# The second product of a feed forward as seven products of quarters

## The chip, the cores and the metric

The kernel runs on one core of a Trainium2 chip. The metric is the device time of one execution in microseconds. The engines are PE (matrix products), DVE (vector), ACT (scalar), POOL (GpSimd) and SP, which here only issues transfers; an engine that issues a transfer does so from a queue of its own.

## The reference

Two decoder layers on 512 tokens of 1024 channels. Each has three token mixers (pooling, an S5 state space, sparse attention), a merge, a layer norm, and then the feed forward, whose last two lines are what most of the change touches:

```python
for i in range(DEPTH):        # DEPTH = 2
    proj = x @ w_in           # then pool_mixer, s5_mixer, nsa_mixer on parts of proj
...
x = layer_norm(ALPHA * x + merged @ w_out, ln1_g, ln1_b)
h = jnp.square(jax.nn.relu(x @ w_ff1)) @ w_ff2      # 1024 -> 4096 -> 1024
return layer_norm(ALPHA * x + h, ln2_g, ln2_b)
```

Everything is in fp32.

## The kernel before, in words

An fp32 product is made of three matmuls of a shorter type. Each operand is split into a high part, rounded by a cast, and a low part, the remainder; `mm3_` (L98 to L100) sums high x high, high x low and low x high in PSUM. So each matrix costs a cast on ACT and a subtraction on DVE before PE can take it, and each 128x512 piece of a result costs three matmuls per 128 channels that are summed over.

Weights come through `wload` (L69 to L87): SP loads 512 KB into a staging tile `wst` (2 buffers), ACT casts it to `wh` (L82), DVE subtracts to get `wl` (L85); `wh` and `wl` have 4 buffers each. PSUM has 8 banks: `mm` 3, `s` 2, `t` 2, `o` 1.

The feed forward (`ffn` L1093, `feed_forward` L1224) goes through the 4096 hidden channels in 8 chunks of 512. `up(c)` makes the four hidden tiles of a chunk: 24 matmuls each, relu on ACT, square on DVE (L1103), split on ACT and DVE (`hi_lo`, L61, L62). `down(c)` multiplies the chunk with its 512 rows of the second weight matrix: for each half of the output channels and each block of 128 tokens `part` makes 12 matmuls and DVE adds the tile into the running sum `xs` (L1120). The loop issues `up(c + 1)` ahead of `down(c)`, and so PE always has products of the one or the other kind. The last chunk is done block by block, with the layer norm of a finished block beside the products of the next.

A tile framework puts each engine's instructions into an order of its own, by priorities; after that an engine executes in order, and each instruction waits for its operands and its buffers by semaphores.

Beside the feed forward of layer 0 stand two preparations for layer 1. `s5_ahead` (L535) lets POOL compute the operands of layer 1's S5 stage and store them to DRAM in four blocks `s5d`, one for each r; `wload` fetches the first four weights of layer 1's input projection at chunk 2. At the start of layer 1, `front(r)` in `s5_` loads a block back into `zwe` and transposes it on PE (L589). It is a generator that is advanced between other work: the number that it yields (L584: 10 for the first block, 3 for the others) says how many steps of the projection go ahead of it. A step is three matmuls.

Of the kernel before, what the change touches and what calls it, by code (L numbers as in the profile page):

```python
# [9 lines left out]
F32 = mybir.dt.float32  # L10
R = mybir.dt.float32r
# [7 lines left out]
DEPTH = 2  # L19
# [7 lines left out]
class Kern:  # L27
# [40 lines left out]

    def wload(self, ap, pool=None, split=None):  # L69
# [421 lines left out]
    def s5_operands(self, pool, i, r, zwe, eng, alone=False):  # L491
# [43 lines left out]
    def s5_ahead(self, i, after):  # L535

        with self.tc.tile_pool(name=f"s5a{i}", bufs=1, reuse_waits="tile") as pool:
            qs = [self.t(pool, [128, 3328], F32, f"zwe{k}") for k in range(2)]
            for r in range(5):
                with self.tc.issue_after(after):  # L540
                    if r < 2:
                        self.nc.gpsimd.memset(qs[r][:, 0:2304], 0.0)
                    if r < 4:
                        self.s5_operands(pool, i, r, qs[r % 2], self.nc.gpsimd, True)
                if r:
                    with self.tc.issue_after(self.loaded):
                        self.nc.sync.dma_start(self.s5d[r - 1], qs[(r - 1) % 2])
                yield

    def s5_(self, i):  # L550
# [5 lines left out]
        with tc.tile_pool(name=f"s5{i}", bufs=1, reuse_waits="tile") as sp:  # L556
# [21 lines left out]
            def front(r):  # L578
# [4 lines left out]
                Km = Ks[r % 2]  # L583
                yield 3 if r else 10  # L584
                lqs = []
# [506 lines left out]

    def ffn(self, i, xs, p0):  # L1093

        nc, v = self.nc, self.nc.vector

        def up(c):
            hs = []
            for m in range(4):
                ps = p0[m] if c == 0 else self.xw([self.wload(self.A["wf1"][i, 4 * c + m])])[0]  # L1100
                h = self.t(self.mt, [128, 512], F32, "mt")
                nc.scalar.activation(h, ps, AF.Relu)
                v.tensor_tensor(h, h, h, OP.mult)  # L1103
                hh, hl = self.pair("ab"[c % 2])
                self.hi_lo(hh, hl, h)
                hs.append((hh, hl))
            return hs

# [21 lines left out]
        def down(c, hs, post):  # L1130
            W = self.A["wf2"]
            if c < 7:
                for half in range(2):
                    ws = [None] * 4
                    for kp in range(2):
                        ws[2 * half + kp] = self.wload(W[i, c, half, kp])
                    for tb in range(4):
                        part(hs, ws, tb, half, c)
            else:
                ws = [self.wload(W[i, c, half, kp]) for half in range(2) for kp in range(2)]  # L1140
                return blocks(hs, ws, post)
# [82 lines left out]
    def feed_forward(self, i, xs, p0, w0p, g, b):  # L1224
        nc, A = self.nc, self.A
        up, down = self.ffn(i, xs, p0)
        how = ("aa", "aa", "am", "vv")
# [13 lines left out]
        for c in range(8):  # L1241
            nx = up(c + 1) if c < 7 else None
            if c == 1 and i < DEPTH - 1:
                ahead = self.s5_ahead(i + 1, self.affine.ins)
            if 1 <= c < 7 and i < DEPTH - 1:
# [9 lines left out]
            block = down(c, hs, post)  # L1255
            hs = nx
        if i < DEPTH - 1:
# [101 lines left out]
```

## Time and profile before

| what | us |
|---|---|
| median of 3 runs | 1772.05 |
| lowest and highest | 1771.15, 1772.34 |
| the profiled execution | 1768.97 |
| its span | 1767.2 |
| layer 0's feed forward | about 565 to 905 |
| layer 1's feed forward | about 1413 to 1751 |

The profile has the busy time of each engine, the chain of work that ended last, groups of instructions by line and form, what an engine waited for, and busy times by windows of the span. Matmuls are pipelined: one starts before the one ahead of it has ended, so the mean time of one is longer than the step from one to the next.

### The profile page before, as it was taken

To read this page: it belongs to the slowest core of one execution; us is meant where nothing else is said; L and a number is where in the kernel's file an instruction comes from. 1 tells how busy PE (TensorE), PEld (TensorE's weight loads), DVE (VectorE), ACT (ScalarE), POOL (GpSimd) and SP (SyncE) were. 2 spreads that over 40 slices of the span, in tenths; PEclk is the share of its full clock that TensorE was granted. 3 is DMA by queue.
4 is the path that set the end of the run, shared out by engine and by line. 5 is a ranking of instruction groups with operands and counts; after the bars stand their busy time and mean duration, and the time that the engine had idled before them with its cause. 6 is when DMAs were issued, how large, how long until landed. Compare 5 with 4: busy or idle time off the path is not lost.

```text
span 1767.2 us, 22544 instructions
## 1 busy us (share of the span) xinstructions
PE 1672.5 (95%) x8356; PEld 1397.7 (79%) x8356; DVE 1135.8 (64%) x2171; ACT 711.8 (40%) x1245; POOL 546.2 (31%) x636
## 2 busy tenths in 40 slices
PE   3969999999999999999998999999999999999996
PEld 2857887887779888888897788878787888888885
DVE  8797568676578656444576565867657774444447
ACT  2444336666534323233242442555564433222221
POOL 4993421322113999400033233122202050000002
PEclk9989999999999999999998999999999999999998
DMA  5313251111251246443316424211124133333331
GB/s 193 117 37 98 87 184 60 57 51 60 87 188 36 93 143 190 138 139 97 113 61 205 164 88 150 87 60 60 56 88 161 43 119 96 96 97 100 101 97 59
DMA packets 64334, 183.69 MB, mean 104 GB/s; under 512 B 12256, under 2 KB 21216, under 8 KB 63200
## 3 DMA queue, kind: packets, MB, share of 16 engines
q1 hardware_dynamic: 61632, 176.88, 30.9%
q10 hardware_dynamic: 2592, 5.38, 1.0%
q8 instruction: 65, 1.06, 0.3%
q14 instruction: 45, 0.37, 0.1%
HBM read 164.93 MB, written 17.30 MB: 103 GB/s over the span
## 4 chain that ended last, share of the span: by engine, by line
PE 78%; DVE 12%; POOL 4%; DMA 3%; ACT 2%; issue 1%; SPq 0%; DVEq 0%; ACTq 0%; POOLq 0%
PE mm L98 16%; PE mm L99 16%; PE mm L100 16%; PE s L99 4%; PE s L100 4%; PE s L98 4%; PE t L99 3%; PE t L100 3%; PE t L98 3%; PE o L834 3%; PE t L929 2%; DVE wl L85 1%; PE s L901 1%; PE s L900 1%; PE o L801 1%
## 5 line engine op out<-in xcount | busy, mean ns | idle before, releaser
L82 ACT CAST wh<-wst 128x1024 fp32r<-128x1024 f32 (+1 forms) x260 | 270.4, 1042 | 545.7 <-PE s L100 210.9
L85 DVE TENSOR_TENSOR wl<-wst,wh 128x1024 fp32r<-128x1024 f32 (+2 forms) x212 | 281.0, 1327 | 253.0 <-ACT wh L82 252.6
L98 PE MATMUL mm<-xh,wh 128*128 128x512 f32 (+1 forms) x1088 | 429.8, 395 | 6.6 <-ACT wh L82 5.4
L100 PE MATMUL mm<-xh,wl 128*128 128x512 f32 (+1 forms) x1088 | 420.2, 386 | 7.5 <-DVE wl L85 7.5
L99 PE MATMUL mm<-xl,wh 128*128 128x512 f32 (+1 forms) x1088 | 419.1, 385 | 0.0
L100 PEld LDWEIGHTS mm<-xh,wl 128*128 128x128 f32 x1088 | 205.5, 189 | 50.1 <-DVE wl L85 8.8
L98 PEld LDWEIGHTS mm<-xh,wh 128*128 128x128 f32 x1088 | 205.8, 189 | 44.9 <-ACT wh L82 5.9
L99 PEld LDWEIGHTS mm<-xl,wh 128*128 128x128 f32 x1088 | 206.0, 189 | 33.8
L85 POOL TENSOR_TENSOR wl<-wst,wh 128x1024 fp32r<-128x1024 f32 x48 | 122.2, 2546 | 239.2 <-ACT wh L82 233.5
L193 POOL TENSOR_TENSOR xm<-xm,ln_g 128x512 f32<-128x512 f32 x9 | 12.2, 1367 | 321.2 <-ACT xm L192 321.2
L906 ACT ACTIVATE P<-P,mx 128x512 f32<-128x512 f32 (+3 forms) x128 | 71.3, 559 | 63.5 <-DVE mx L904 63.0
L904 DVE CUSTOM_DVE_ANT_0 P<-s,mask 128x512 f32<-128x512 f32 (+3 forms) x128 | 59.6, 484 | 45.3 <-PE s L901 38.1
L62 DVE TENSOR_TENSOR Pl<-t,Ph 128x384 fp32r<-128x384 f32 (+1 forms) x96 | 57.3, 597 | 35.8 <-ACT Ph L61 35.5
L1120 DVE TENSOR_TENSOR xm<-xm,t 128x512 f32<-128x512 f32 x56 | 38.4, 686 | 54.1 <-PE t L100 51.2
L222 POOL TENSOR_TENSOR xm<-xm,hi_a 128x512 f32<-128x512 f32 x8 | 12.7, 1585 | 180.5 <-PE t L238 180.5
L222 POOL TENSOR_TENSOR xm<-xm,ln_g 128x512 f32<-128x512 f32 x16 | 30.2, 1886 | 121.6 <-PE t L238 121.6
L1120 DVE TENSOR_TENSOR xm<-xm,s 128x512 f32<-128x512 f32 x56 | 38.2, 682 | 41.6 <-PE s L100 41.6
L913 POOL TENSOR_SCALAR P<-P,sm,gate 128x128 f32<-128x128 f32 x32 | 15.3, 479 | 156.2 <-DVE sm L908 156.2
L61 ACT CAST Ph<-t 128x384 fp32r<-128x384 f32 (+1 forms) x96 | 48.1, 505 | 26.2 <-PE t L929 26.1
L98 PE MATMUL mm<-hi_a,wh 128*128 128x512 f32 x132 | 54.7, 414 | 2.1 <-DVE lo_a L318 2.1
L1103 DVE TENSOR_TENSOR mt<-mt 128x512 f32<-128x512 f32 x64 | 55.6, 869 | 0.0
L929 PE MATMUL t<-ident,P 128*128 128x128 f32 x320 | 51.8, 276 | 2.7 <-DVE P L913 2.7
(406 smaller groups left out, 3834.3 us busy)
## 6 DMA issues: line engine op xcount, KB each, us to landing
wst<-in_wf_dram SPq DMA_DIRECT2D x128, 512.0 KB, 3.5
wst<-in_win_dram SPq DMA_DIRECT2D x80, 512.0 KB, 3.3
wst<-in_wup_dram SPq DMA_DIRECT2D x24, 512.0 KB, 3.5
wst<-in_wout_dram SPq DMA_DIRECT2D x16, 512.0 KB, 4.2
s5d<-zwe SPq DMA_DIRECT2D x4, 1664.0 KB, 9.2
zwe<-s5d SPq DMA_DIRECT2D x4, 1664.0 KB, 9.1
xd<-xm SPq DMA_DIRECT2D x8, 512.0 KB, 4.9
w<-in_w_dram SPq DMA_DIRECT2D x8, 512.0 KB, 7.6
```

Of the source, the lines that this page charges most:

```text
L62: b = self.nc.vector.tensor_tensor(lo, src, hi.bitcast(F32), OP.subtract)
L82: self.nc.scalar.copy(wh, st)
L85: e.tensor_tensor(wl, st, wh.bitcast(F32), OP.subtract)
L98: mm(out, ah, bh, start=first and i == 0, stop=False, **kw)
L99: mm(out, ah, bl, start=False, stop=False, **kw)
L100: mm(out, al, bh, start=False, stop=last and i == n - 1, **kw)
L834: mm = lambda o, a, b, **k: nc.tensor.matmul(o, a, b, skip_group_check=True, **k)
L904: v.tensor_tensor_reduce(out=p, in0=ss[qb], in1=self.mask[:, 384 - 128 * qb:512], scale=-1.0, scalar=3e38, op0=OP.add, op1=OP.min, accum_o ...
L906: nc.scalar.activation(p, p, AF.Exp, bias=mx[:, qb:qb + 1], scale=-1.0, accum_out=c)
L929: nc.tensor.transpose(pt[:, n:n + 128], P[:, c:c + 128], self.ident)
L1103: v.tensor_tensor(h, h, h, OP.mult)
L1120: v.tensor_tensor(r, r, ps, OP.add)
```

## The change

A chunk that is `fast` (chunks 0 to 6 of layer 1; 0, 5 and 6 of layer 0) computes `down` as a product of 2x2 blocks in the seven products of Strassen's scheme in Winograd's form. The blocks of the hidden activations are quarters (256 channels x 256 tokens in two pieces of 128 channels), the blocks of the weights are the four loaded pieces. Four sums of the weights and four of the activations are formed on DVE in fp32 and then split; each product goes to two PSUM tiles, and DVE adds them into `xs` and into two tiles `AU`, which hold a term that three of the four output quarters have in common and are added to those at chunk 6. The raw weight pieces stay in four buffers of `big`, and are summed in place there.

Besides, the square of the hidden tile moves from DVE to ACT in all chunks. Twelve weights (the last chunk's four in both layers, the first four of layer 1's input projection) get `wl` in another way (`sums=True`): ACT writes the negated weight to it, rounded as in `wh`, and a transfer on POOL's queue adds the exact weight from DRAM, which leaves the remainder. The small S5 loads and the S5 stores of `s5_ahead` go from SP's to POOL's queue, in four steps instead of six. The first four weights of layer 1 are loaded at chunk 7. The affine part of the layer norm takes the blocks in another order, and the first S5 block of layer 1 yields 18 instead of 10.

```diff
     def wload(...)
+            if sums:
+                self.nc.scalar.activation(wl, st, AF.Copy, scale=-1.0)
+                self.nc.gpsimd.dma_start(wl, ap, accum_op=OP.add)
+                return wh, wl
...
-            for r in (rs[3], rs[0], rs[1], rs[2]):
+            for r in (rs[3], rs[2], rs[0], rs[1]):
...
-        nc.sync.dma_start(bc, self.A["s5bc"][i, :, :, r * 64:(r + 1) * 64])
+        (gl if alone else nc.sync).dma_start(bc, self.A["s5bc"][i, :, :, r * 64:(r + 1) * 64])
...
+                    self.nc.gpsimd.dma_start(self.s5d[r], qs[r % 2])
...
-                yield 3 if r else 10
+                yield 3 if r else 18 if i else 10
...
+        fast = lambda c: c < 7 and (i == DEPTH - 1 or c in (0, 5, 6))
+        def hidden(c, m, h):
+            ps = p0[m] if c == 0 else self.xw([self.wload(self.A["wf1"][i, 4 * c + m])])[0]
+            nc.scalar.activation(h, ps, AF.Relu)
+            nc.scalar.activation(h, h, AF.Square)
...
+            p11, p12, p22 = (split(q, self.pair("ab"[c % 2])) for q in (a11, a12, a22))
+            v.tensor_tensor(a22, a22, a21, OP.subtract)
+            e1 = esplit(a22, 1)
+            v.tensor_tensor(a21, a11, a21, OP.subtract)
+            v.tensor_tensor(a11, a11, a22, OP.add)
+            v.tensor_tensor(a12, a11, a12, OP.subtract)
+            e4 = esplit(a12, 4)
+            e3 = esplit(a21, 3)
+            e2 = esplit(a11, 2)
...
+        def products(c, hs):
...
+                b11, b12, b21, b22 = load(0, 0), load(1, 0), load(0, 1), load(1, 1)
+                w11 = split(b11)
+                add(b11, b12)
+                t1 = split(b11)
+                w21 = split(b21)
+                w22 = split(b22)
+                add(b12, b22)
+                t3 = split(b12)
+                add(b11, b22)
+                t2 = split(b11)
+                add(b11, b21)
+                t4 = split(b11)
...
+            mul(p11, w11, A)
+            if c == 0:
+                for j in range(2):
+                    v.tensor_copy(AU[j], A[j])
+            else:
+                acc(u, A, plus)
+            mul(e1, t1, C)
+            acc(lambda j: r(3, j), C, minus)
+            mul(p12, w21, A, False)
+            acc(lambda j: r(0, j), A, plus)
+            mul(e4, w22, C, False)
+            acc(lambda j: r(1, j), C, minus)
+            D, B = [self.psum("o"), self.psum("s")], [self.psum("s"), self.psum("t")]
+            mul(e3, t3, D)
+            acc(lambda j: r(3, j), D, minus)
+            mul(e2, t2, B)
+            acc(u, B, minus)
+            mul(p22, t4, D, False)
+            acc(lambda j: r(2, j), D, plus)
...
-            if c == 2 and i < DEPTH - 1:
-                w0 = [self.wload(A["win"][i + 1, j], w0p, nc.vector) for j in range(4)]
+            if c == 7 and i < DEPTH - 1:
+                w0 = [self.wload(A["win"][i + 1, j], w0p, sums=True) for j in range(4)]
...
+            if c == 6:
+                self.w7 = [self.wload(A["wf2"][i, 7, half, kp], w7, sums=True) for half in range(2) for kp in range(2)]
```

`load` brings a raw piece into `big` over SP, `split` casts on ACT and subtracts on DVE, `mul` makes 12 matmuls into two PSUM tiles (with `False` on top of what is there), and `acc` adds two tiles.

DVE in the middle of layer 1's feed forward, before: splits of weights (`wl`, 1024 columns), additions of tiles to `xm` (the tiles of `xs`), and a square and a remainder for each hidden tile.

```order
L85 TENSOR_TENSOR wl_14656<-wst_14653,wh_14655 128x1024
L85 TENSOR_TENSOR wl_14694<-wst_14691,wh_14693 128x1024
L1103 TENSOR_TENSOR mt_14570<-mt_14570 128x512
L62 TENSOR_TENSOR lo_a_14574<-mt_14570,hi_a_14573 128x512
L85 TENSOR_TENSOR wl_14700<-wst_14697,wh_14699 128x1024
L1103 TENSOR_TENSOR mt_14608<-mt_14608 128x512
L62 TENSOR_TENSOR lo_a_14612<-mt_14608,hi_a_14611 128x512
L85 TENSOR_TENSOR wl_14762<-wst_14759,wh_14761 128x1024
```

The same place now, around the start of a chunk's products; L1158 is a split of a weight block or sum, L1161 a sum of weight blocks, L1187 an accumulation.

```order
L1158 TENSOR_TENSOR wl_14330<-wh_14316,wh_14329 128x1024
L1161 TENSOR_TENSOR wh_14316<-wh_14316,wh_14322 128x1024
L62 TENSOR_TENSOR lo_a_14285<-wl_14150,hi_a_14284 128x512
L1158 TENSOR_TENSOR wl_14334<-wh_14320,wh_14333 128x1024
L1158 TENSOR_TENSOR wl_14338<-wh_14322,wh_14337 128x1024
L1187 TENSOR_TENSOR au_2500_13170<-au_2500_13170,s_14356 128x512
L1187 TENSOR_TENSOR au_2501_13171<-au_2501_13171,s_14357 128x512
L62 TENSOR_TENSOR lo_a_14289<-wl_14217,hi_a_14288 128x512
L62 TENSOR_TENSOR lo_a_14293<-wl_14217,hi_a_14292 128x512
L1187 TENSOR_TENSOR xm_12491<-xm_12491,t_14358 128x512
L1158 TENSOR_TENSOR wl_14343<-wh_14318,wh_14342 128x1024
```

The squares are gone, and sums and accumulations stand between the splits.

SP over one chunk in the same stretch, before: four loads of the first weight matrix, four of the second, all into `wst`.

```order
L79 DMA wst_2672_14251<-in_wf1_dram 128x1024
L79 DMA wst_2679_14289<-in_wf1_dram 128x1024
L79 DMA wst_2686_14327<-in_wf1_dram 128x1024
L79 DMA wst_2693_14365<-in_wf1_dram 128x1024
L79 DMA wst_2700_14403<-in_wf2_dram 128x1024
L79 DMA wst_2703_14409<-in_wf2_dram 128x1024
L79 DMA wst_2710_14471<-in_wf2_dram 128x1024
L79 DMA wst_2713_14477<-in_wf2_dram 128x1024
```

Now, the loads of one chunk:

```order
L79 DMA wst_2751_14463<-in_wf1_dram 128x1024
L79 DMA wst_2755_14496<-in_wf1_dram 128x1024
L1152 DMA wh_2782_14628<-in_wf2_dram 128x1024
L1152 DMA wh_2783_14630<-in_wf2_dram 128x1024
L1152 DMA wh_2784_14632<-in_wf2_dram 128x1024
L1152 DMA wh_2785_14634<-in_wf2_dram 128x1024
L79 DMA wst_2760_14530<-in_wf1_dram 128x1024
L79 DMA wst_2764_14563<-in_wf1_dram 128x1024
```

The four loads of the second matrix go to four buffers of their own, and stand between the second and the third load of the first matrix.

PE at the first S5 block of layer 1, before: `mm` tiles are the projection, `t` the transposes of `zwe`.

```order
L100 MATMUL mm_8657<-xh_1552_8024,wl_8654 128x512
L98 MATMUL mm_8657<-xh_1552_8024,wh_8653 128x512
L99 MATMUL mm_8657<-xl_1553_8025,wh_8653 128x512
L100 MATMUL mm_8657<-xh_1552_8024,wl_8654 128x512
L589 MATMUL t_8664<-ident_81,zwe_1613_8573 128x128 x4
```

Now:

```order
L103 MATMUL mm_8753<-xl_1587_8121,wh_8749 128x512
L104 MATMUL mm_8753<-xh_1586_8120,wl_8750 128x512
L102 MATMUL mm_8799<-xh_1584_8118,wh_8795 128x512
L103 MATMUL mm_8799<-xl_1585_8119,wh_8795 128x512
L104 MATMUL mm_8799<-xh_1584_8118,wl_8796 128x512
L590 MATMUL t_8806<-ident_81,zwe_1645_8669 128x128 x4
```

Before, one tile of 24 matmuls and 6 of the next (`mm_8657`) stand between the 128x256 products and the transposes; now two tiles (`mm_8753` the second) and 6 of the third (`mm_8799`).

## Rows read from the trace of the kernel before

**Rows 1.** The page, busy time of the engines and the chain that ended last.

```profile
PE 1672.5 (95%) x8356; PEld 1397.7 (79%) x8356; DVE 1135.8 (64%) x2171; ACT 711.8 (40%) x1245; POOL 546.2 (31%) x636
...
PE 78%; DVE 12%; POOL 4%; DMA 3%; ACT 2%; issue 1%; SPq 0%; DVEq 0%; ACTq 0%; POOLq 0%
```

**Rows 2.** Windows: stretch, length, busy us of PE, PEld, DVE, ACT, POOL, clock, DMA.

```profile
609.00:652.00 43.00, 43.00 (x191) 35.59 (x191) 21.47 (x24) 12.58 (x16) 42.17 (x77) 1.00 0.31 99
1413.00:1751.00 338.00, 337.98 (x1535) 281.41 (x1534) 178.33 (x222) 100.42 (x128) 30.59 (x19) 1.00 0.30 94
```

**Rows 3.** Instructions by form, PE, 1460 to 1740 us: busy, mean ns, idle before.

```profile
L98 PE MATMUL mm<-xh,wh 128*128 128x512 f32 x192 | 74.7, 389 | 0.0
```

**Rows 4.** Timeline of PE, layer 1's feed forward: start us, duration us.

```profile
1534.28 0.39 PE L99 MATMUL t<-wl,hi_a 128*128 128x512 f32 x1
...
1535.87 0.39 PE L100 MATMUL t<-wh,lo_a 128*128 128x512 f32 x1
```

**Rows 5.** Instructions by form, DVE, 1460 to 1740 us.

```profile
L85 DVE TENSOR_TENSOR wl<-wst,wh 128x1024 fp32r<-128x1024 f32 x51 | 62.4, 1223 | 84.7 <-ACT wh L82 84.7
L1120 DVE TENSOR_TENSOR xm<-xm,t 128x512 f32<-128x512 f32 x26 | 17.9, 687 | 26.9 <-PE t L100 26.5
...
L62 DVE TENSOR_TENSOR lo_b<-mt,hi_b 128x512 fp32r<-128x512 f32 x12 | 8.3, 692 | 6.2 <-ACT hi_b L61 6.2
```

**Rows 6.** Timeline of DVE, three instructions that follow on each other.

```profile
1544.18 1.23 DVE L85 TENSOR_TENSOR wl<-wst,wh 128x1024 fp32r<-128x1024 f32 x1 [1.76 <-ACT wh L82]
1545.32 0.68 DVE L1120 TENSOR_TENSOR xm<-xm,s 128x512 f32<-128x512 f32 x1
1545.92 1.22 DVE L85 TENSOR_TENSOR wl<-wst,wh 128x1024 fp32r<-128x1024 f32 x1
```

**Rows 7.** Instructions by form, ACT, 1460 to 1740 us.

```profile
L82 ACT CAST wh<-wst 128x1024 fp32r<-128x1024 f32 x50 | 52.7, 1054 | 159.0 <-PE s L100 100.6 <-PE mm L99 58.4
L1102 ACT ACTIVATE mt<-mm 128x512 f32<-128x512 f32 x24 | 14.1, 589 | 0.0
L61 ACT CAST hi_b<-mt 128x512 fp32r<-128x512 f32 x12 | 7.5, 622 | 16.8 <-DVE mt L1103 16.8
```

**Rows 8.** Instructions by form, DVE and POOL, 609 to 690 us in layer 0.

```profile
L85 DVE TENSOR_TENSOR wl<-wst,wh 128x1024 fp32r<-128x1024 f32 x18 | 24.8, 1377 | 23.3 <-ACT wh L82 23.3
...
L1120 DVE TENSOR_TENSOR xm<-xm,t 128x512 f32<-128x512 f32 x7 | 4.8, 683 | 6.3 <-PE t L100 4.1 <-POOL Wc L463 2.1
...
L62 DVE TENSOR_TENSOR lo_b<-mt,hi_b 128x512 fp32r<-128x512 f32 x4 | 3.3, 818 | 0.0
...
L461 POOL TENSOR_TENSOR ct<-Wc,s_are 128x128 f32<-128x128 f32 x6 | 4.7, 777 | 0.2
```

**Rows 9.** DMA issues: KB each, median us from issue to landing.

```profile
wst<-in_wf_dram SPq DMA_DIRECT2D x128, 512.0 KB, 3.5
...
s5d<-zwe SPq DMA_DIRECT2D x4, 1664.0 KB, 9.2
```

**Rows 10.** Windows, a stretch of dense loads; share and GB/s stand last.

```profile
240.00:254.00 14.00, 14.00 (x64) 11.58 (x63) 13.67 (x23) 3.47 (x6) 4.36 (x6) 1.00 0.97 337
```

**Rows 11.** What PE waited for, 900 to 1100 us: total, times, longest.

```profile
PE t L589 <- DMA zwe<-s5d: 5.8, 1, 5.8
```

**Rows 12.** Timeline of PE around the first S5 transposes of layer 1.

```profile
932.33 0.39 PE L100 MATMUL mm<-xh,wl 128*128 128x512 f32 x1
938.54 1.97 PE L589 MATMUL t<-ident,zwe 128*128 128x128 f32 x8 [5.82 <-DMA zwe<-s5d]
```

**Rows 13.** Windows behind that gap; the granted clock is third from last.

```profile
935.00:940.00 5.00, 1.46 (x7) 1.46 (x8) 2.19 (x4) 0.31 (x1) 3.23 (x2) 0.56 1.00 414
940.00:945.00 5.00, 5.00 (x27) 3.84 (x26) 1.04 (x3) 1.96 (x4) 0.00 (x0) 0.76 0.52 154
```

**Rows 14.** What DVE waited for, 1460 to 1740 us.

```profile
DVE lo_b L62 <- ACT hi_b L61: 6.2, 9, 0.7
```

More of the change, by code (lines that the diff above doesn't have):

```diff
@@ L67, in hi_lo_scaled, with wload @@
         self.nc.vector.scalar_tensor_tensor(lo, src, scale, hi.bitcast(F32), op0=OP.mult, op1=OP.subtract)
-    def wload(self, ap, pool=None, split=None):
+    def wload(self, ap, pool=None, split=None, sums=False):
         n = ap.shape[1]
@@ L538, in s5_ahead @@
             qs = [self.t(pool, [128, 3328], F32, f"zwe{k}") for k in range(2)]
-            for r in range(5):
+            for r in range(4):
                 with self.tc.issue_after(after):
@@ L542, in s5_ahead @@
                         self.nc.gpsimd.memset(qs[r][:, 0:2304], 0.0)
[L543 to L547, printed above, removed]
+                    self.s5_operands(pool, i, r, qs[r % 2], self.nc.gpsimd, True)
+                    self.nc.gpsimd.dma_start(self.s5d[r], qs[r % 2])
                 yield
@@ L1097, in up @@
         def up(c):
             hs = []
[L1099 to L1107, printed above, removed]
+            if not fast(c):
+                for m in range(4):
+                    h = self.t(self.mt, [128, 512], F32, "mt")
+                    hidden(c, m, h)
+                    hh, hl = self.pair("ab"[c % 2])
+                    self.hi_lo(hh, hl, h)
+                    hs.append((hh, hl))
+                return hs
@@ new lines, in up, with split @@
+            for k in range(2):
+                q = by2(self.t(big, [128, 1024], R, "wl", 4).bitcast(F32))
+                for m in range(2):
+                    hidden(c, 2 * k + m, q[:, m])
+                hs.append(q)
+            f = slice(0, 256), slice(256, 512)
+            a11, a12, a21, a22 = hs[0][:, :, f[0]], hs[1][:, :, f[0]], hs[0][:, :, f[1]], hs[1][:, :, f[1]]
+            def split(src, pair):
+                hh, hl = (by2(q) for q in pair)
+                self.hi_lo(hh, hl, src)
+                return hh, hl
@@ new lines, in esplit @@
+            def esplit(src, n):
+                return split(src, [self.t(fp, [128, 512], R, f"e{n}{x}") for x in "hl"])
+            p11, p12, p22 = (split(q, self.pair("ab"[c % 2])) for q in (a11, a12, a22))
[5 more added lines that the diff above has]
+            e4 = esplit(a12, 4)
@@ new lines, in up, with load, split, mul @@
+            e3 = esplit(a21, 3)
+            e2 = esplit(a11, 2)
+            return p11, p12, p22, e1, e2, e3, e4
+        def products(c, hs):
+            p11, p12, p22, e1, e2, e3, e4 = hs
+            W = self.A["wf2"]
+            def load(half, kp):
+                x = self.t(big, [128, 1024], R, "wh", 4).bitcast(F32)
+                self.loaded = nc.sync.dma_start(x, W[i, c, half, kp]).ins
+                return x
+            def split(x):
+                wh, wl = (self.t(self.wp, [128, 1024], R, q, 4) for q in ("wh", "wl"))
+                nc.scalar.copy(wh, x)
+                v.tensor_tensor(wl, x, wh.bitcast(F32), OP.subtract)
+                return wh, wl
+            add = lambda a, b: v.tensor_tensor(a, a, b, OP.add)
+            with self.tc.high_priority():
+                b11, b12, b21, b22 = load(0, 0), load(1, 0), load(0, 1), load(1, 1)
[10 more added lines that the diff above has]
+                t4 = split(b11)
+            r = lambda n, j: xs[2 * (n // 2) + j][:, (n % 2) * 512:(n % 2 + 1) * 512]
+            def mul(a, w, ps, first=True):
+                for j in range(2):
+                    s = slice(j * 128, (j + 1) * 128)
+                    terms = [((a[0][:, k, s], a[1][:, k, s]), (w[0][:, k * 512:(k + 1) * 512], w[1][:, k * 512:(k + 1) * 512])) for k in range(2)]
+                    self.mm3(ps[j], terms, first=first, skip=True)
+            def acc(dst, ps, op):
+                for j in range(2):
+                    with self.tc.high_priority():
+                        v.tensor_tensor(dst(j), dst(j), ps[j], op)
+            u, minus, plus = lambda j: AU[j], OP.subtract, OP.add
+            A, C = [self.psum("s") for j in range(2)], [self.psum("t") for j in range(2)]
+            mul(p11, w11, A)
+            if c == 0:
+                for j in range(2):
+                    v.tensor_copy(AU[j], A[j])
[15 more added lines that the diff above has]
+            if c == 6:
+                for j in range(2):
+                    for n, op in ((1, minus), (2, plus), (3, minus)):
+                        v.tensor_tensor(r(n, j), r(n, j), AU[j], op)
@@ L1131, in down @@
             W = self.A["wf2"]
-            if c < 7:
+            if fast(c):
+                products(c, hs)
+            elif c < 7:
                 for half in range(2):
@@ L1139, in down @@
             else:
-                ws = [self.wload(W[i, c, half, kp]) for half in range(2) for kp in range(2)]
+                ws = self.w7
                 return blocks(hs, ws, post)
@@ L1225, in feed_forward, with feed @@
         nc, A = self.nc, self.A
-        up, down = self.ffn(i, xs, p0)
+        with ExitStack() as stack:
+            fp = stack.enter_context(self.tc.tile_pool(name=f"ff{i}", bufs=1, reuse_waits="tile"))
+            self.feed(i, xs, p0, w0p, g, b, fp, stack)
+    def feed(self, i, xs, p0, w0p, g, b, fp, stack):
+        nc, A = self.nc, self.A
+        up, down = self.ffn(i, xs, p0, w0p, fp)
         how = ("aa", "aa", "am", "vv")
@@ L1256, in feed_forward @@
             hs = nx
+            if c == 5 and i == DEPTH - 1:
+                w7 = w0p
+            elif c == 5:
+                next(ahead, None)
+                w7 = stack.enter_context(self.tc.tile_pool(name=f"w7{i}", bufs=1, reuse_waits="tile"))
+            if c == 6:
+                self.w7 = [self.wload(A["wf2"][i, 7, half, kp], w7, sums=True) for half in range(2) for kp in range(2)]
         if i < DEPTH - 1:
```

6 lines of the change are left out of this document (4 added, 2 removed).

## The prediction

> **What bounds the kernel now.** I read the page first, then the windows of the feed forward, then the rows of single instructions there, and last the waits of the matrix engine. The page [rows 1] gives PE 95% of the span and DVE 64%; the chain that ended last runs over PE for 78% and over DVE for 12%. The windows say where this matters [rows 2]: from 1413 to 1751 us, the whole feed forward of layer 1, PE is busy for 337.98 of 338 us at full clock, with DVE at 53% and ACT at 30%; in layer 0 the stretch 609 to 652 reads 43.00 of 43.00. So a matmul that is left out in a feed forward is time saved, as long as nothing else comes late there.
>
> What one matmul costs must not be taken from its mean. The row of the up product gives 389 ns [rows 3], but matmuls overlap: eight successive starts go from 1534.28 to 1535.87 [rows 4], 7 steps in 1.59 us, or 0.227 us each. That is the price of one removed.
>
> The profiled execution took 1768.97 us, 3.1 us below the median of the three runs, 1772.05. Durations are from the first; I subtract differences from the second. A difference of 0.2%, 3.5 us, is about the least that can be told from none.
>
> **The matmuls that go.** A chunk of the second product was 8 tiles of 12 matmuls, 96; as seven products of quarters it is 7 x 12 = 84. Ten chunks change, seven in layer 1 and three in layer 0: 120 x 0.227 = **27.2 us** less PE time. A chunk's period falls from 192 to 180 matmuls, 43.5 to 40.8 us, 2.7 us each. By the 389 ns mean it would be 47 us, which I reject, since the steps are what PE advances by.
>
> **What DVE gets for it.** Per chunk of layer 1 DVE had 8 splits of 1024 columns and 16 operations of 512. It now has 15 of 1024 (11 splits, 4 weight sums) and 25 of 512 (7 remainders, 4 combinations of the hidden quarters, 14 accumulations); the four squares go to ACT. With the row means, 1.223 and 0.687 us [rows 5], that is 15 x 1.223 + 25 x 0.687 = 35.5 us of the 40.8, 87%. Back to back the starts lie closer: 1.14 us after a 1024 and 0.60 after a 512 [rows 6], and so 32.1 us, 79%. The squares on ACT cost 4 x 0.59, the row of the relu, and with 11 casts of 1.054 and 7 of about 0.6 [rows 7] ACT comes to 21 us, half of the period; I take that as hidden.
>
> So nothing is full, but DVE executes in order, and the work is uneven. I went through one chunk of the order with t = 0 at its first product. DVE waits about 1.2 us for ACT's cast of w22, and then has 6 operations of 1024 and 18 of 512 before the remainder of the weight that the next up product needs. PE asks for it after 88 matmuls, at 19.9 us. By the start steps DVE has it at 1.2 + 6 x 1.14 + 18 x 0.60 = 18.8, in time by 1.1; by the row means at 1.2 + 7.3 + 12.4 = 20.9, late by 1.0. Between the two I take 0.5 us late per chunk, in nine chunks: **+4.5** (0 to 9). In the other places of a chunk (a PSUM tile read before its second product, the remainders of e1 to e4) I find between 1.3 and 3 us in hand.
>
> The tenth is chunk 0 of layer 0, which runs beside POOL's work for the next layer's S5 (POOL busy 42.17 of 43 us [rows 2]). There a split takes 1.377 us for 1.223 and a remainder 0.818 for 0.692, while an accumulation out of PSUM keeps 0.683 [rows 8]. The 17.6 us of steps grow by an eighth, to about 20: **+1.4** once (0 to 3). The Trainium skill, "SBUF — State Buffer", section "Who interferes with whom", has DVE operations with two SBUF inputs contend with a GpSimd instruction that reads SBUF, as an exclusive lock. It speaks against placing products here: were each of the 15 splits and sums blocked for one such instruction, 0.777 us in the same rows, the chunk would need up to 12 us more. The split's mean of 1.377 agrees with the contention and not with that size.
>
> **Loads.** SP now holds the four raw weight blocks of a chunk as one burst, which waits until the fourth sum is split (its buffers are those blocks), and the next up product's third and fourth weights queue behind it. The split ends at 1.2 + 5 x 1.14 + 16 x 0.60 = 16.5. One 512 KB load lands 3.5 us after its issue [rows 9], and a burst moves 337 GB/s [rows 10], 1.56 us per load. The fifth then lands at 16.5 + 3.5 + 4 x 1.56 = 26.2 and is split by 28.5; PE needs it after 84 + 48 matmuls, at 29.9. Hidden with 1.4 us to spare: **0**, and the slower rival below if not.
>
> Twelve weights (the last chunk's four in each layer, and the four of layer 1's first projections) take their remainder from ACT and an adding transfer on the POOL queue in place of a DVE split. No row shows such a transfer. The nearest are the 512 KB load, 3.5 us, and the 1664 KB store, 9.2 us [rows 9]; the former has its size, so I take it. The tightest, the fourth of layer 1's last chunk, has 7.8 us between its issue and PE's need, so it costs **0** (with 9.2 us, 1.4; no gain, since PE had no wait there). The Trainium skill, "DMA: Bandwidth & Descriptors", section "Anatomy of one DMA", has 2.0 us plus the bytes over 436e3 for such a queue, an estimate of 3.2 us here; no run shows it, and the sum would be the same. The S5 stores and small loads that move from SP to POOL finish some 200 us before they are read: 0. The first four weights move from chunk 2 to chunk 7 of layer 0, where over 10 us stand in front of their use: 0.
>
> **The S5 stage.** Before, PE waits 5.8 us for the first S5 block of layer 1 [rows 11]: it stops after 932.33 and starts again at 938.54 [rows 12]. With eight more steps the transposes come one projection later, behind 24 more matmuls of 512 columns, 24 x 0.227 = 5.4 us. Both the load's place on SP and what it follows are unchanged, so its landing is, too. The wait falls to 0.4: **-5.4**. After the gap the granted clock was 0.56 and then 0.76 [rows 13], in 1.46 and 5 us of work, so (0.44 x 1.46 + 0.24 x 5) = 1.8 us at most was lost to the lower of the two levels; later gaps remain and may take it, so I count a third: **-0.6** (0 to -1.8). If the landing moves with the transposes, this part gives 0.
>
> **Sum.** 1772.05 - 27.2 - 5.4 - 0.6 + 4.5 + 1.4 = 1744.8, **1745 us**. With its own bounds (DVE 0 to 9, clock, the S5 wait unhelped) it spans 1740 to 1751.
>
> **Rivals.**
>
> *Nothing comes late.* DVE keeps to its start steps everywhere: 1772.05 - 27.2 - 6.0 = 1739. For it: 79% of the period by steps. The Trainium skill, "Perfetto Trace Analysis", section "Identifying the Most-Contended Engine", calls occupancy a fair measure for Vector; by that rule an engine below 100% costs nothing, and this is the time. Against it: the phase of products alone needs 18.8 of 19.9 us. Chance 0.15.
>
> *DVE's order is the bound.* Beyond the row means (1.0 late) two of the phase's remainders wait for ACT, 0.7 us each as they do now (9 waits, 6.2 us [rows 14]), and each chunk loses 2.4: 9 x 2.4 = 21.6 where I put 4.5, so 1762. For it: seven casts of the chunk and four relus share ACT with the splits. Against: ACT is half idle. Chance 0.20.
>
> *Slower: the loads behind the burst.* The up product's third weight lands late. It decides from 3.3 us per chunk, where ten chunks have eaten the 33 us: 16.5 + 5x + 2.3 - 29.9 = 3.3 gives x = 2.9 us per load. At 3.1, between 1.56 and 3.5, a chunk loses 4.4: 1772.05 - 33.2 + 44 = 1783. For it: two staging buffers, one queue in order, and a later split moves the whole burst. Against: the bandwidth of [rows 10] holds over 14 us. Chance 0.10.
>
> *The S5 move does nothing*, and a wait as long stands one projection later: 1745 + 6 = 1751. Chance 0.07.
>
> **How the numbers follow.** The forecast, 1745 with 1740 to 1752, has 0.45; the four rivals 0.52; 0.03 is left for what I have not seen. The range 1737 to 1765 takes in the forecast, the S5 case, nearly all of the full gain and three quarters of the DVE case, about 0.8. Faster by over 0.2%: the forecast, the S5 case, the full gain, the DVE case, 0.87, less a little for worse mixtures: 0.86. Within 0.2%: 0.05, a loss of 3 us per chunk. Slower: 0.09.
>
> **What would show it.** Right: chunk starts 41 to 41.5 us apart in layer 1, DVE at 80 to 87% there, PE waits of about 0.5 us on the weight remainder (line 89) once per chunk, no wait on the adding transfers, the S5 wait under 1 us. Wrong: PE waiting on ACT's or DVE's weights in the third up tile (the loads), PE waits on DVE in several places of a chunk that sum over 2 us (DVE), a wait of 5 us on the S5 block, or a period of 43 us or more.

## The result and the profile after

The changed kernel takes 1746.97 us, the median of 4 runs (1744.01 to 1749.18), against 1772.19 for the kernel before: 25.2 us less, a ratio of 0.9859 with an interval of 0.9843 to 0.9875. Run once more, beside other kernels of the study, it took 1746.57. The forecast was 1745. The total is right, but its terms are not, and that is what the rest is about.

The page of the changed kernel, first the busy times, then the chain:

```profile
PE 1649.1 (94%) x8236; PEld 1377.4 (79%) x8236; DVE 1238.6 (71%) x2307; ACT 807.4 (46%) x1381; POOL 557.5 (32%) x656
...
PE 75%; DVE 14%; POOL 3%; DMA 3%; ACT 3%; issue 2%; SPq 0%; ACTq 0%; DVEq 0%; POOLq 0%
```

Against [rows 1] PE has 23 us less to do, DVE 103 us more, ACT 96 us more. The profiled execution took 1749.18 us, 2.2 over its median, and the one of before 3.2 under; so the two traces differ by 19.8 us only. A count of stages shows where. Three places that both kernels have serve as landmarks besides the last matmul: the last group of transposes of `xm` ahead of layer 0's feed forward, the first group ahead of layer 1, and the first group ahead of layer 1's feed forward. The timeline of PE before (start, duration):

```profile
555.64 0.60 PE L238 MATMUL t<-ident,xm 128*128 128x128 f32 x4
...
892.39 0.60 PE L238 MATMUL t<-ident,xm 128*128 128x128 f32 x4
...
1392.06 0.71 PE L238 MATMUL t<-ident,xm 128*128 128x128 f32 x5
...
1750.75 0.39 PE L100 MATMUL mm<-wh,lo_b 128*128 128x512 f32 x1
```

and of the changed kernel:

```profile
556.21 0.49 PE L242 MATMUL t<-ident,xm 128*128 128x128 f32 x3
...
892.08 0.60 PE L242 MATMUL t<-ident,xm 128*128 128x128 f32 x4
...
1393.29 0.38 PE L242 MATMUL t<-ident,xm 128*128 128x128 f32 x2
...
1732.93 0.39 PE L104 MATMUL mm<-wh,lo_b 128*128 128x512 f32 x1
```

| stage, by these starts | before | after | difference |
|---|---|---|---|
| up to the first landmark | 555.64 | 556.21 | +0.6 |
| layer 0's feed forward, 555.64 to 892.39, and 556.21 to 892.08 | 336.75 | 335.87 | -0.9 |
| layer 1 up to its feed forward, to 1392.06, and to 1393.29 | 499.67 | 501.21 | +1.5 |
| layer 1's feed forward up to the last matmul | 358.69 | 339.64 | -19.05 |
| from there to the end of the span (1767.2, 1747.4) | 16.45 | 14.47 | -2.0 |

In layer 1's feed forward the 84 removed matmuls come to 19.0 us, as the step says. In layer 0, 36 removed matmuls bring 0.9 us and not 8.2, and the stage with the S5 block (layer 1 up to its feed forward) nothing in this execution. That stage varies: in the second profiled execution of the same kernel (1745.03 us) it took 494.65, 5.0 less than before, while layer 0's feed forward took 337.59.

**Layer 1.** The starts of the products of two chunks in succession:

```profile
1529.16 0.39 PE L102 MATMUL s<-wh,hi_a 128*128 128x512 f32 x1
...
1569.96 0.39 PE L102 MATMUL s<-wh,hi_b 128*128 128x512 f32 x1
```

They lie 40.80 us apart, 180 steps of 0.2267, as from each chunk's start to the next, 0 to 6. The windows, columns as in [rows 2], have PE without a gap and DVE at 82%:

```profile
1528.00:1685.00 157.00, 157.00 (x694) 130.00 (x693) 129.56 (x159) 79.48 (x104) 1.55 (x2) 1.00 0.35 109
```

The deadline that the forecast worked on is the weight remainder that the next up product needs, forecast at 18.8 us after the start of the products and asked for at 19.9. On DVE and PE:

```profile
1546.82 1.22 DVE L89 TENSOR_TENSOR wl<-wst,wh 128x1024 fp32r<-128x1024 f32 x1
...
1549.11 0.39 PE L104 MATMUL mm<-xh,wl 128*128 128x512 f32 x1
```

The split begins 17.66 us after 1529.16, ends at 18.88, and PE takes it at 19.95. The rows of DVE (columns as in [rows 5]) have the durations of before, in more instructions:

```profile
L1158 DVE TENSOR_TENSOR wl<-wh,wh 128x1024 fp32r<-128x1024 f32 x48 | 58.6, 1221 | 38.8 <-ACT wh L1157 38.8
L1161 DVE TENSOR_TENSOR wh<-wh,wh 128x1024 f32<-128x1024 f32 x27 | 33.0, 1223 | 0.6
...
L1187 DVE TENSOR_TENSOR xm<-xm,t 128x512 f32<-128x512 f32 x26 | 17.8, 683 | 0.1
```

**Layer 0.** What PE waited for from 560 to 900 us, where the kernel before waited for nothing:

```profile
PE o L102 <- DVE xm L1187: 3.5, 1, 3.5
PE mm L102 <- ACT hi_b L61: 0.6, 1, 0.6
PE s L102 <- DVE au L1194: 0.4, 1, 0.4
```

The large one stands at 871.69, in the products of chunk 6. ACT's timeline there, and behind it DVE's and PE's:

```profile
863.67 1.05 ACT L82 CAST wh<-wst 128x1024 fp32r<-128x1024 f32 x1
870.24 1.06 ACT L84 ACTIVATE wl<-wst 128x1024 fp32r<-128x1024 f32 x1 [5.52 <-DMA wst<-in_win_dram]
871.20 1.03 ACT L82 CAST wh<-wst 128x1024 fp32r<-128x1024 f32 x1
872.14 1.04 ACT L1157 CAST wh<-wh 128x1024 fp32r<-128x1024 f32 x1
...
873.21 1.23 DVE L1158 TENSOR_TENSOR wl<-wh,wh 128x1024 fp32r<-128x1024 f32 x1 [5.18 <-ACT wh L1157]
874.35 0.68 DVE L1187 TENSOR_TENSOR xm<-xm,o 128x512 f32<-128x512 f32 x1
...
875.18 0.47 PE L102 MATMUL o<-wh,hi_a 128*128 128x512 f32 x1 [3.49 <-DVE xm L1187]
```

ACT stood 5.52 us in front of a pass over a weight that had not landed, the third of layer 1's first projections (L84). Behind it in the queue stood the cast of the last weight sum of chunk 6 (L1157 at 872.14), which DVE splits and PE multiplies with next. DVE stood 5.18 us in front of that split, with an accumulation behind it (874.35) that the same product needs, and so PE's wait is put down to the accumulation. The load came late in a stretch in which transfers filled the queues. The windows have a DMA share of 1.02 in the 10 us before the stall, and behind it a granted clock of 0.66 of 2.4 GHz, that is part of the 5 us at the lower level of 1.2 GHz:

```profile
860.00:870.00 10.00, 10.00 (x45) 8.26 (x46) 8.03 (x11) 4.72 (x6) 0.89 (x1) 1.00 1.02 255
870.00:875.00 5.00, 1.69 (x8) 1.07 (x6) 1.79 (x3) 4.43 (x5) 1.34 (x2) 1.00 0.39 47
875.00:880.00 5.00, 4.82 (x14) 3.87 (x15) 4.90 (x9) 0.51 (x1) 0.41 (x1) 0.66 1.04 240
```

The transfers by issue:

```profile
wst<-in_wf_dram SPq DMA_DIRECT2D x88, 512.0 KB, 3.5
...
s5d<-zwe POOLq DMA_DIRECT2D x4, 1664.0 KB, 6.7
...
wl<-in_wf_dram POOLq DMA_DIRECT2D x8, 512.0 KB, 6.9
...
wl<-in_win_dram POOLq DMA_DIRECT2D x4, 512.0 KB, 8.2
```

The adding transfers (`wl`, on POOL's queue) took 6.9 and 8.2 us, where I had taken 3.5. The 6.9 is a median over both layers; the four of layer 1 alone, in the window 1640 to 1725 us, took 5.5, and the four of layer 0 took 8.6:

```profile
wl<-in_wf_dram POOLq DMA_DIRECT2D x4, 512.0 KB, 5.5
```

The estimate of 3.2 us by the Trainium skill ("DMA: Bandwidth & Descriptors", section "Anatomy of one DMA") is further off. The measured values decide; the eight in layer 0 ran where the queues were full, and plain loads of the first projections' weights took 6.9 there as well.

**The S5 stage.** The wait of 5.8 us on the block, [rows 11], is 0.5. The block itself comes no later: its transposes start 46.15 us behind the landmark before and 46.30 after, as the forecast had assumed. But other waits are new:

```profile
PE mm L102 <- ACT gate L723: 5.9, 1, 5.9
PE mm L103 <- DVE wl L89: 3.5, 1, 3.5
...
PE t L590 <- DMA zwe<-s5d: 0.5, 1, 0.5
```

### The profile page after: what moved, and what is told of

It reads as the page before. It is cut to its first block, busy times and chain, and to the rows that moved or that the text cites. A ratio compares the mean times of both kernels' runs of the same rounds, so it can differ in the third digit from the quotient of the medians.

```text
span 1747.4 us, 22631 instructions
## 1 busy us (share of the span) xinstructions
PE 1649.1 (94%) x8236; PEld 1377.4 (79%) x8236; DVE 1238.6 (71%) x2307; ACT 807.4 (46%) x1381; POOL 557.5 (32%) x656
## 4 chain that ended last, share of the span: by engine, by line
PE 75%; DVE 14%; POOL 3%; DMA 3%; ACT 3%; issue 2%; SPq 0%; ACTq 0%; DVEq 0%; POOLq 0%
PE mm L102 16%; PE mm L103 16%; PE mm L104 16%; PE s L103 3%; PE s L104 3%; PE s L102 3%; PE o L835 3%; PE t L930 2%; PE t L104 2%; PE t L103 2%; PE t L102 2%; DVE wl L89 1%; ACT wh L82 1%; PE s L902 1%; PE s L901 1%
## 5 line engine op out<-in xcount | busy, mean ns | idle before, releaser
L82 ACT CAST wh<-wst 128x1024 fp32r<-128x1024 f32 (+2 forms) x220 | 228.0, 1039 | 363.8 <-PE mm L103 138.7
L89 DVE TENSOR_TENSOR wl<-wst,wh 128x1024 fp32r<-128x1024 f32 (+2 forms) x160 | 214.4, 1343 | 164.2 <-ACT wh L82 163.5
L1158 DVE TENSOR_TENSOR wl<-wh,wh 128x1024 fp32r<-128x1024 f32 x70 | 87.5, 1250 | 62.2 <-ACT wh L1157 62.2
L85 POOL DMA_DIRECT2D wl<-in_wf_dram x8 | 7.1, 885 | 385.7 <-PE mm L103 243.0
L1157 ACT CAST wh<-wh 128x1024 fp32r<-128x1024 f32 x70 | 73.6, 1051 | 110.7 <-PE mm L103 57.0
L226 POOL TENSOR_TENSOR xm<-xm,ln_g 128x512 f32<-128x512 f32 x16 | 26.7, 1669 | 121.5 <-PE t L242 121.5
L104 PE MATMUL mm<-hi_a,wl 128*128 128x512 f32 x132 | 53.2, 403 | 0.0
L103 PE MATMUL mm<-lo_a,wh 128*128 128x512 f32 x132 | 52.9, 401 | 0.0
```

What stands on the lines that cost most here:

```text
L103: mm(out, ah, bl, start=False, stop=False, **kw)
L104: mm(out, al, bh, start=False, stop=last and i == n - 1, **kw)
L1157: nc.scalar.copy(wh, x)
L1158: v.tensor_tensor(wl, x, wh.bitcast(F32), OP.subtract)
```

## Experiments

Each time is the median of a kernel's runs, taken beside runs of the kernel before on the same chip, whose own median there was 1771.0 to 1772.8.

### Layer 0 without products

```diff
-        fast = lambda c: c < 7 and (i == DEPTH - 1 or c in (0, 5, 6))
+        fast = lambda c: c < 7 and i == DEPTH - 1
```

> Edit: the changed kernel with no fast chunk in layer 0, 36 matmuls more. Theory A (the three chunks of layer 0 save 8.2 us of matmuls and lose about 7 of it at the end of chunk 6, 3.5 us of a wait and some 2.6 us of a lower clock behind it): 1747 plus 1, so 1747 to 1749, and no wait over 1 us on PE between 860 and 890 us. Theory B (the 8.2 us come through, as forecast less the 1.4): 1754 to 1755.

Measured: 1744.53 (1742.01 to 1751.64). That is 2.5 below theory A's range and 9.5 below theory B's, so nearer to A, and no worse than with the three chunks; layer 0's feed forward takes 336.8 us by the landmarks, as before the change, and PE has no wait in it. The three chunks of layer 0 were worth nothing as they stood.

### ACT's queue at the end of chunk 6

```diff
-                w0 = [self.wload(A["win"][i + 1, j], w0p, sums=True) for j in range(4)]
+                w0 = []
+                for j in range(4):
+                    with ExitStack() as order:
+                        if j >= 2:
+                            order.enter_context(self.tc.issue_after(self.cast))
+                        w0.append(self.wload(A["win"][i + 1, j], w0p, sums=True))
```

(`self.cast` is the cast of the last weight sum.) It moves that cast ahead of the passes over the third and fourth weight, and nothing else on ACT.

> Edit: the changed kernel with the third and fourth weight of layer 1's first projections queued on ACT behind the cast of the last product's weights of layer 0's chunk 6. Theory A (ACT's queue: that cast stands behind a pass over a weight that has not landed): the wait of 3.5 us at 872 us goes and the clock with it, 1747 less 6, so 1741. Theory B (the transfers are the limit, with the DMA share at 1.0 from 860 to 870 us, and the cast waits for something else, or the first projections then wait for their weights): 1746 to 1748.

Measured: 1742.09 (1739.76 to 1744.97), about 4.7 below the changed kernel (1746.97 and 1746.57), against 6 expected; by the landmarks layer 0's feed forward goes from 335.9 to 329.2, which is 6.7. That 2 us of it do not reach the whole time stays open. On ACT the cast now stands ahead of the passes over the late weight:

```profile
865.48 1.05 ACT L1157 CAST wh<-wh 128x1024 fp32r<-128x1024 f32 x1 [1.61 <-DVE wh L1161]
869.66 1.06 ACT L82 CAST wh<-wst 128x1024 fp32r<-128x1024 f32 x1 [3.13 <-DMA wst<-in_win_dram]
```

The wait of PE is gone, and 329.2 is 0.6 above what 36 matmuls less would give (336.75 - 8.16 = 328.6). The transfers were as many as before, with a DMA share of 0.92 from 860 to 870 us, and the weight lands at 869.66, against 870.24. So the order on ACT made the stall, theory A.

### Without the adding transfers

```diff
-                w0 = [self.wload(A["win"][i + 1, j], w0p, sums=True) for j in range(4)]
+                w0 = [self.wload(A["win"][i + 1, j], w0p, nc.vector) for j in range(4)]
...
-                self.w7 = [self.wload(A["wf2"][i, 7, half, kp], w7, sums=True) for half in range(2) for kp in range(2)]
+                self.w7 = [self.wload(A["wf2"][i, 7, half, kp], w7, nc.vector) for half in range(2) for kp in range(2)]
```

> Edit: the changed kernel with the twelve weights split on DVE, not by ACT and an adding transfer: 12 operations of 1.22 us more on DVE, 12 of 1.05 us fewer on ACT, 6.3 MB fewer transfers. Theory A (the adding transfers and ACT's second pass make the stall at the end of layer 0's chunk 6, DVE has room there): 1741 to 1743, with no wait over 1 us between 860 and 890. Theory B (DVE is what is short at chunk 6, which the adding transfers were to relieve): new PE waits on DVE there and in layer 1's chunk 6, 1749 or more.

Measured: 1741.30 (1738.87 to 1743.56). The same stretch, in one window of this kernel:

```profile
860.00:880.00 20.00, 20.00 (x90) 16.58 (x89) 19.27 (x29) 3.06 (x3) 0.00 (x0) 1.00 0.22 67
```

PE has no gap, and the DMA share is 0.22; layer 0's feed forward takes 329.2 here too. Theory A holds, by the time and by layer 0. In layer 1 the adding transfers do earn something: without them 16.5 us lie between the last matmul and the end, as in the kernel before; with them it is 14.5, in the changed kernel and in the kernel without products below. This is the 2.0 us of the table above that no term of the forecast had. The traces show where they lie. DVE's last accumulation (L1226) starts 2.55 us after the last matmul in the changed kernel and 4.57 in this one, and from there to the end both take 11.9. Ahead of it stand short steps of the layer norm (L157, L163) that take 0.16 to 0.22 us alone. Beside a two-input instruction of POOL such a step lasts until that instruction ends, and more of them meet POOL in this kernel (POOL's line holds two instructions):

```profile
1720.34 2.53 POOL L199 TENSOR_TENSOR xm<-xm,ln_b 128x512 f32<-128x512 f32 x2
...
1720.43 1.21 DVE L163 SCALAR_TENSOR_TENSOR ln_y<-ln_y 128x1 f32<-128x1 f32 x1
1721.68 1.21 DVE L157 SCALAR_TENSOR_TENSOR ln_y<-ln_y 128x1 f32<-128x1 f32 x1
```

That DVE comes to them later because it has four splits more ahead of them is likely, but was not tried.

### The products taken out, all else kept

```diff
-        fast = lambda c: c < 7 and (i == DEPTH - 1 or c in (0, 5, 6))
+        fast = lambda c: False
```

> Edit: the changed kernel with no fast chunk at all; all its other edits stay. Theory A (the products bring the 19.0 us of layer 1's 84 matmuls and about 1 us in layer 0, and the other edits the remaining 5 of the 25): 1766 to 1768. Theory B (the products bring all of it and the other edits nothing): 1771 to 1773.

Measured: 1763.77 (1759.01 to 1765.42), ratio 0.9946 (0.9931 to 0.9961): below both. The products bring 17 us and the other edits 8. Of these 2 are the tail; the other 6 are the size that was forecast for the S5 stage, though the one profile of this kernel has only 2.0 of them there (497.7 for 499.7).

### The S5 move, with and without the products

```diff
-                yield 3 if r else 18 if i else 10
+                yield 3 if r else 10
```

> Edit: the changed kernel with the first S5 block of layer 1 ten steps in, as before. Theory A (the S5 move only shifts the wait: in the changed kernel's profile the 5.8 us wait on the S5 block became 0.5, but 3.5 us on a weight remainder and 5.9 us behind ACT's gate are new): no change against the changed kernel's 1747, so 1745 to 1749, and a wait of 5 to 6 us on the S5 block again. Theory B (the forecast: the move is worth the 6 us): 1753.

Measured: 1747.46 (1745.01 to 1748.52): no change. The waits of this kernel:

```profile
PE t L590 <- DMA zwe<-s5d: 5.7, 1, 5.7
PE s L641 <- POOL Si L632: 2.2, 1, 2.2
```

The block's 5.7 us are back, and the 5.9 and 3.5 us of the changed kernel are gone. That is theory A. But the opposite edit on the kernel before (10 to 18) says otherwise:

> Edit: the kernel before with the first S5 block of layer 1 eighteen steps in. Theory A (the wait only moves): 1770 to 1773, no difference from the kernel before. Theory B (the move is worth 6 us where the kernel before had its 5.8 us wait): 1766.

Measured: 1764.26 (1761.92 to 1769.23), ratio 0.9959 (0.9944 to 0.9973), 7.6 us less (4.8 to 9.9 by that interval): theory B. It has the new waits as well:

```profile
PE mm L98 <- ACT gate L722: 5.5, 1, 5.5
PE mm L99 <- DVE wl L85: 2.3, 1, 2.3
PE t L589 <- DMA zwe<-s5d: 0.9, 1, 0.9
```

So the move was measured twice more, in kernels with the stall of layer 0 mended, and beside them the changed kernel again.

> Edit: none, the changed kernel on the same chip as the two below. Both theories: 1744 to 1749, which was its span of times. It is the mark from which the worth of the S5 move is read, since that move gave 0.5 us in the changed kernel (first kernel of the study) and 7.6 in the kernel before.

> Edit: the kernel with ACT's queue held (1742.1), with the first S5 block ten steps in. Theory A (with the products the move is worth nothing): 1741 to 1744. Theory B (it is worth the 6 to 8 us that it gave the kernel before, and the first comparison was blurred by the spread of single executions, some 5 us): 1747 to 1750.

> Edit: the kernel with all chunks of layer 0 fast and ACT's queue held (1737.5), with the first S5 block ten steps in. Theory A: 1736 to 1739. Theory B: 1743 to 1746.

Measured: 1746.57, 1742.83 and 1739.88. The changed kernel repeats its time. With ten steps the two are 0.7 and 2.4 us slower than with eighteen (1742.09, and 1737.53 in the section on all fourteen chunks). The first is theory A; the second is 0.9 over theory A's range and 3.1 under theory B's. So:

| kernel | 10 steps | 18 steps | worth of the move |
|---|---|---|---|
| before, no products | 1771.9 | 1764.3 | 7.6 |
| the change | 1747.5 | 1747.0 | 0.5 |
| with ACT's queue held | 1742.8 | 1742.1 | 0.7 |
| that, and all chunks of layer 0 | 1739.9 | 1737.5 | 2.4 |

By the landmarks of the profiles, layer 1 up to its feed forward takes 499.3 to 501.5 us with ten steps, four profiles. With eighteen it takes 492.6, 495.6 and 497.7 where layer 0 has no products, and 494.7 to 501.2 in seven profiles where it has. The move exchanges a wait of 5.3 to 6.0 on the block for two later ones, of 5.0 to 6.1 behind ACT's gate and of 1.8 to 3.5 on a weight remainder. The latter is 1.8 to 2.3 in the three kernels without products in layer 0, and 2.5 to 3.5 in the seven with them. So products in layer 0 seem to take part of the move's worth away; only a part of the difference between 7.6 and 0.5 to 2.4 is seen in these waits, the three small values are within the spread of one kernel's runs, and what makes the remainder late stays open.

### How much DVE has in hand

In the products of layer 1's chunks 1 to 6, n operations that nothing reads:

```diff
+            if i == DEPTH - 1 and c:
+                with self.tc.high_priority():
+                    for _ in range(n):
+                        v.tensor_tensor(DM, AU[0], AU[1], OP.add)
             mul(p12, w21, A, False)
```

With n = 4:

> Edit: the changed kernel with four more operations of 512 columns on DVE (a sum of the two AU tiles into a scratch tile that nothing reads) in the products of chunks 1 to 6 of layer 1. Theory A (DVE's order has 1.1 us in hand, the profile has the remainder at 18.88 and PE asking at 19.95): 4 x 0.60 is 2.4, late by 1.3 in each of the five chunks that have a next up product of their own, so 6 to 8 us slower than the changed kernel, 1753 to 1755, and PE waits on line 89 of about 1.3 us. Theory B (what counts is the share of busy time, 5 us of each 40.8 are free): 1747.

Measured: 1762.62 (1760.32 to 1763.32), about 16 over the changed kernel, twice what theory A had. With n = 2:

> Edit: the kernel with added work on DVE, with two operations of 512 columns in place of four. With four, PE waited 0.79 us on the weight remainder of the fifth product and 0.21 twice on ACT's casts, and a chunk took 42.9 us for 40.8. Theory A (DVE's order has about 1.1 us in hand): two add 1.2 us, all but used up, so chunks of 40.8 to 41.3 us and at most 3 us of the matmuls' time lost; with some 2 us more behind the last matmul, 1747 to 1752. Theory B (any work added to DVE is paid in full, half of the 15.8 us that four cost): 1754 to 1756.

Measured: 1756.99 (1752.06 to 1757.90), 10 over the changed kernel, above both ranges. What PE waited for in layer 1's chunks, first with two, then with four:

```profile
PE o L103 <- DVE wl L1159: 5.1, 5, 1.0
```

```profile
PE o L103 <- DVE wl L1159: 3.9, 5, 0.8
PE mm L102 <- ACT wh L82: 2.1, 10, 0.2
```

The starts of two chunks in succession are 42.34 and 42.88 us apart. So 1.2 us of added work cost 1.5 per chunk and 2.4 cost 2.1. The deadline that is missed is not the one of the forecast but that of the split of the fourth sum (`t4`). In the changed kernel it ends 16.55 us into the products and PE asks for it at 17.68, so 1.1 us are in hand there too. With two operations it ends at 18.95, 2.4 later: 1.2 are the added work, and 1.2 come from the order, since the framework put a remainder (`e3l`) and an accumulation ahead of it that stood behind it. PE is there at 17.7 and starts 1.3 late. With four it ends 3.0 later, as only the remainder moved ahead, and PE waits on two of ACT's casts as well. Behind the last matmul, four operations cost 4.5 us more, 18.9 for 14.5; two cost nothing there (14.5). The window of the kernel with four:

```profile
1528.00:1685.00 157.00, 152.19 (x658) 122.18 (x657) 131.97 (x169) 71.55 (x94) 0.00 (x0) 1.00 0.32 101
```

DVE is busy for 84% of it. So the idle share is not free, against theory B of the kernel with four, and the fall is steeper than theory A had for both. Theory B of the kernel with two, that all work is paid, comes nearest in size, 10 against 8, but four operations do not cost twice what two do in a chunk.

### All fourteen chunks

```diff
-        fast = lambda c: c < 7 and (i == DEPTH - 1 or c in (0, 5, 6))
+        fast = lambda c: c < 7
```

on top of the kernel with ACT's queue held.

> Edit: the third kernel of this study (ACT's queue held) with all seven chunks of layer 0 fast too, 48 matmuls less. Theory A (DVE beside POOL's S5 work keeps pace as in chunk 0, which lost 0.4 to 0.8 us): 1742 less 10.9 plus 4 times 0.6, so 1733 to 1735. Theory B (splits and sums stretched beside POOL, 1.377 for 1.223, make each of chunks 1 to 3 late, or the S5 preparation is late): 1740 or more.

Measured: 1737.53 (1732.93 to 1739.62), ratio 0.9801 (0.9783 to 0.9820), the fastest kernel of the study and 9 us below the changed one. The gain over the kernel with three chunks is 4.6, not 8.5: by the landmarks layer 0's feed forward goes from 329.2 to 325.9. Its chunks start 42.41, 41.81, 42.96, 42.25, 41.99 and 40.80 us apart. Those beside POOL's S5 work are 1.0 to 2.2 us longer than 40.80, the one behind it is not, and PE's waits there are all on DVE (2.4 us in six waits). DVE's rows from 600 to 760 us say why:

```profile
L1158 DVE TENSOR_TENSOR wl<-wh,wh 128x1024 fp32r<-128x1024 f32 x25 | 34.9, 1398 | 11.2 <-ACT wh L1157 11.2
...
L1161 DVE TENSOR_TENSOR wh<-wh,wh 128x1024 f32<-128x1024 f32 x15 | 19.5, 1303 | 0.3
L1187 DVE TENSOR_TENSOR xm<-xm,t 128x512 f32<-128x512 f32 x16 | 10.8, 675 | 0.0
```

Splits take 1.398 us in the mean, against 1.221 in layer 1, and accumulations out of PSUM 0.675, no more than there. Singly, the splits take 1.21 to 2.02 us. The longest starts beside an instruction of POOL and ends 1.1 us, about a split's own length, after that one:

```profile
687.14 1.03 POOL L465 TENSOR_TENSOR et<-zwe,s_pr 128x512 f32<-128x512 f32 x1
...
687.24 2.02 DVE L1158 TENSOR_TENSOR wl<-wh,wh 128x1024 fp32r<-128x1024 f32 x1
```

This is theory B in kind, since each chunk beside POOL is late, with a size between the two.

## Why the prediction was right, and where it was not

**The matmuls: right, by the step.** 0.2267 us each and not 0.389: 19.05 measured in layer 1 for 84.

**DVE: right in the ledger, wrong in the choice.** "Between the two I take 0.5 us late per chunk" was the step that failed: chunks start 40.80 us apart and not 41 to 41.5, and PE never waits on line 89 in layer 1's feed forward. The start steps gave 18.8 and the trace has 18.88; the row means were never real, because a duration overlaps the next start by 0.08. So +4.5 was 0 in layer 1, and there the rival in which nothing comes late was the right one. Its reason is not: with four operations more DVE is busy for 84%, and PE pays 2.1 us per chunk. The Trainium skill ("Perfetto Trace Analysis", section "Identifying the Most-Contended Engine") calls occupancy a fair measure of how close Vector is to its limit; these runs do not bear out what the rival made of it, that an engine below 100% costs nothing, since here a deadline is missed at 84%. "Between 1.3 and 3 us in hand" elsewhere in the chunk was a little too much: the split of the fourth sum has 1.1.

**Chunk 0 of layer 0:** +1.4 forecast. In the changed kernel the next chunk starts 41.44 us later, +0.64, with a wait of 0.4; with ACT's queue held it was 40.80. With all chunks fast it is +1.6, and 1.0 to 2.2 in the others beside POOL's work, so the size was right there. The Trainium skill ("SBUF — State Buffer", section "Who interferes with whom") lets two-input operations contend and those out of PSUM not; the rows agree on both. The forecast set the mean against its exclusive lock, and that was a wrong reading: 14% is a mean over splits that meet POOL and splits that do not, and the longest single one, 0.8 us over, is lengthened by about one of POOL's instructions.

**The adding transfers: wrong.** "The tightest, the fourth of layer 1's last chunk" was the wrong place to look. There the four were in time. At the end of layer 0's chunk 6 eight of them and eight loads meet, they are paid twice (a second pass on ACT, a second transfer on full queues), and the cast behind the pass was late: 3.5 us of wait, another 0.6 before it, and, as the difference that is left, some 2.5 us of slower steps around both, part of them at the lower clock. With the 0.64 of chunk 0 these are the 7.3 that layer 0 lost (335.87 against 328.6).

**The S5 stage: right in size for the kernel before, not for this one.** -6.0 was forecast, and the move alone gives 7.6 there; in the changed kernel, 0.5. So the rival with a chance of 0.07 came nearest, though the later waits are not on the block. The row on the wait came out as forecast (0.5 us), and looking further than that wait was what I left out: the same stage waits on DVE and ACT afterwards.

**The loads behind the burst:** hidden, as forecast. Layer 1's chunks have no wait on PE at all.

**The tail:** 2.0 us better, in no term.

So that 1745 was right to 2 us is in good part luck: terms of +4.5 and +1.4 for DVE, of which 0.64 occurred, stood for the 6.7 that was lost at chunk 6, and 2 us of tail for part of the S5 stage. With the measured terms in place of the forecast ones (7.3 lost in layer 0, S5 0.5, tail 2.0) the sum is 1749.8. The 2.8 us to 1747.0 are not accounted for; the stage between the feed forwards varied by more than that, 494.65 to 501.21 in two executions of this kernel.

## What to carry to other kernels

Where an engine is dense, lay out one period with start-to-start steps, instruction by instruction, and compare each deadline; the share of busy time and the row means say too little and too much. Then look at the seams between stages with the same care, above all for an instruction that waits for a load and has urgent work queued behind it: here one such pass took back most of what three chunks had gained, and its place in the queue was nearly the whole repair. Price a wait that is removed by removing it alone; it was worth 7.6 us in one kernel and 0.5 to 2.4 in others.

## What the runs showed of the hardware

An interruption of PE costs more than the idle time that the profile gives. A wait of 0.36 us made the chunk 0.64 longer, one of 1.01 made it 1.54 longer. Part of this is how idle time is counted: from the end of the matmul before, 0.39 us after its start, while the next would have started after 0.227; by the starts PE was 0.52 and 1.28 late. The rest is slower steps: the first matmul after the wait shows 0.47 and 0.50 us and not 0.39. After the 3.5 us wait the granted clock was 0.66 in the window from 875 to 880 us.

An adding transfer of 512 KB took 5.5 us in layer 1 and 8.2 to 8.6 at the end of layer 0, where the queues were full; a plain load of that size took 3.5, and 6.9 there.

DVE operations with two inputs in SBUF and POOL's held each other up, one whole instruction at a time: a step of 0.2 us lasted up to 1.21 beside POOL's of 1.26, and a split of 1.22 up to 2.02. Beside the same work the accumulations, with one input in PSUM, kept 0.67 to 0.68.
